# A decoder layer's opening rearranged: dummy matmuls, full-width rotary tables, kept zero columns, an earlier row-scale chain

## The chip, the cores and the metric

One core of a Trainium2 chip runs the kernel, in one launch. The metric is the device time of that launch in microseconds (us), on the core. TensorE (PE in the profile) multiplies matrices and loads their stationary operand (PEld), VectorE (DVE) and ScalarE (ACT) work on tiles of 128 partitions, GpSimd (POOL) fills and copies, and SyncE (SP) issues most transfers. Each engine works through its own instructions in order and waits on semaphores for the others.

## The reference

One layer of a decoder for 256 tokens of width 2048, in fp32, cut to what matters here:

```python
h = rms_norm(x, attn_norm_g)
proj = h @ w_in                               # 2048 x 4480
shifted = h + (prev_token - h) * mu           # of the 3360 columns of the first head group
y_rwkv = rwkv7_mixer(r, k, v, w, a, g, ...)   # 16 heads x 64: a recurrence over tokens
y_mla  = mla_mixer(c_q, c_kv, k_pe, positions, ...)   # 8 heads, a rotary key of 64 columns
x = x + concat(y_rwkv, y_mla) @ w_out
h = rms_norm(x, ffn_norm_g)
x = x + (silu(causal_conv3(h @ w_gate)) * (h @ w_up)) @ w_down     # width 5632
return rms_norm(x, final_norm_g)

def apply_rope(t, positions):
    inv_freq = ROPE_THETA ** (-arange(half) / half)           # half = 32
    ang = positions[..., None] * inv_freq
    return concat([t1 * cos(ang) - t2 * sin(ang), t2 * cos(ang) + t1 * sin(ang)])
```

The recurrence is computed in four chunks of 64 tokens, each with a small triangular system per head.

## The kernel before

**Exact products.** Every fp32 matrix is split into two parts, hi and lo, and the products of the parts are summed. Weights come in pieces of 512 KB. `piece` issues the transfer to a `raw` buffer on SP, ACT casts it to `hi` (L133), DVE subtracts to get `lo` (L134); there are three buffers of each kind. `prod_b` then makes eight matmuls of 512 columns with `hi` (L165: the activations' hi and lo side by side) and eight of 256 columns with `lo` (L168). `in_tile(i)` does this for two pieces and gives 128 columns of the input projection, transposed: 128 columns on partitions, 256 tokens free. `joined` adds the two halves (copy out by ACT L173, add by DVE L174, which frees the accumulator) and multiplies by `rsB`, the RMS norm's row scale (L175), since the matmuls work on x before its norm.

**Order of the projection.** 35 tiles: 0, 25 and 26 first (low-rank inputs, gates, rotary key), then key tiles 1 to 8, r tiles 9 to 16, v tiles 17 to 24, and the latents 27 to 34. Tiles 0, 25, 1 and 3 and most others accumulate in the PSUM pool `mm` (three buffers), 26 in `at` (two), and tile 2 in `ch` (three). So the third key tile, tile 3, needs a `mm` buffer that DVE's L174 must free.

**The opening.** The order of SP's transfers is the written order there (`manual_schedule`); on the other engines a scheduler that simulates the program sets each engine's order when the kernel is built. `xsplit` loads x transposed and splits it; `sums` loads x again and gets the sums of squares (`ssx`, ACT L317). `rsqrt` turns them into the row scale by three Newton steps on DVE (`rm`, `ry`, `rt`, L204 to L216), and `bcast` spreads it over partitions: two diagonal tiles `dg` (DVE L227), two matmuls with `ones` (PE L228, into `rsb`), and a copy to `rsB` (DVE L229). `rope_tables` makes the angles by a careful reduction on DVE (L255 to L281), 64 columns wide with four blocks of 32 frequencies stacked on partitions, takes Sin on ACT (L283 to L285), and 32 GpSimd operations (L291 to L295) spread them to `cosR` and `sinR`, 128 x 256.

**Behind it.** `shifted` joins a tile into a buffer `h` of 257 columns with a zero first column (a GpSimd memset each), and mixes each token with the one before it (ACT L377, DVE L378). `decay` makes the decays of two key tiles with Tanh and Exp (ACT L413 to L420) and a masked scan with `cmask` (DVE L418). When keys and r are there, Gram matrices go to DRAM and come back transposed (`dL`, `Lp`, SP L569), DVE solves the triangular systems row by row (L578 to L588), and the result makes another trip (`dT`, `dU`) to the matmuls `pR` (L628) and `pT` (L641). Projection work fills these waits on PE. Then come the four chunks (`px`, `XB`, `UV`, `pS`, `py`, L677 to L710), attention, the output projection and the FFN, where each of 44 rounds puts a gate tile into `gt`, 258 columns with two zero ones (a memset each).

Of the kernel before, what the change touches and what calls it, by code (L numbers as in the profile page):

```python
# [9 lines left out]
F32 = mybir.dt.float32  # L10
# [7 lines left out]
P = 128  # L18
# [17 lines left out]
    _o += _w  # L36
NVEC = _o

C_ID, C_MK, C_CAUS, C_BLK, C_INVF, NCST = 0, 128, 256, 384, 386, 387


def _two_pi_parts():
# [12 lines left out]
def hybrid_layer(ctx: ExitStack, tc: tile.TileContext, a: dict, out: bass.AP):  # L55
# [11 lines left out]
        uid[0] += 1  # L67
        return f"{s}{uid[0]}"

    NT2, NAT, NS4, NRAW, NHI, NLO, NMM, NCH, NT1 = 3, 2, 21, 3, 3, 3, 3, 3, 7  # L70

    def s4(dt=F32, n="s4"):
        return sb.tile([P, 1024], dt, tag="s4", name=nm(n), bufs=NS4)
# [170 lines left out]
    sinR = con([P, T], "sinR")  # L244

    def rope_tables():
        rp = [t2("rp", 384) for _ in range(2)]
        rp = [u[:, q * 64:(q + 1) * 64] for u in rp for q in range(4)]
        posi = rp.pop().bitcast(I32)
        nc.gpsimd.dma_start(posi, a["pos"])  # L250
        c1, c2, c3, c3r, c4r = _two_pi_parts()
        tpi = 2.0 * math.pi
        ang, k0, kh, lo, w = rp[:5]
        with tc.issue_after(last_x[0]):
            V.tensor_copy(ang, posi)  # L255
# [24 lines left out]
        fms(w, c3r)  # L280
        V.tensor_scalar(ang, ang, 3.1415925, -3.1415925, ALU.min, ALU.max)  # L281
        sn, cn = rp[5:7]
        S.activation(sn, ang, AF.Sin)  # L283
        S.activation(cn, ang, AF.Sin, scale=0.5)
        S.activation(cn, cn, AF.Square)  # L285
        V.tensor_scalar(cn, cn, -2.0, 1.0, ALU.mult, ALU.add)
        for b in range(4):
            bs = slice(b * 32, b * 32 + 32)
            for r in range(4):
                ro = slice(r * 32, r * 32 + 32)  # L290
                nc.gpsimd.tensor_copy(cosR[ro, b * 64:(b + 1) * 64], cn[bs])  # L291
                if r % 2:
                    nc.gpsimd.tensor_copy(sinR[ro, b * 64:(b + 1) * 64], sn[bs])
                else:
                    nc.gpsimd.tensor_scalar(sinR[ro, b * 64:(b + 1) * 64], sn[bs], -1.0, None, ALU.mult)  # L295
# [6 lines left out]

    ones = con([P, P], "ones")
    nc.gpsimd.memset(ones, 1.0)
# [14 lines left out]
    with tc.manual_schedule(engines={mybir.EngineType.SP}):  # L319
# [26 lines left out]
    hkk = con([P, 8], "hkk")
# [16 lines left out]
    with tc.issue_after(dve0):  # L363
        for b in (0, 2):
            V.tensor_copy(cmb[:, b * P:(b + 1) * P], cst[:, C_CAUS:C_CAUS + P])
        V.tensor_copy(idb, ident)
    cmask = t1("cmask")
    nc.gpsimd.memset(cmask, 1.0)
    nc.gpsimd.memset(cmask.rearrange("p (c t) -> p c t", t=64)[:, :, 0:1], 0.0)


    def shifted(acc, i, rows=slice(0, P), dst=None):
        h = t1("h", 257)
        nc.gpsimd.memset(h[rows, 0:1], 0.0)
# [3 lines left out]
        V.scalar_tensor_tensor(o[rows], h[rows, 0:256], vv("mu", i, rows), o[rows], ALU.mult, ALU.add)  # L378
        return o
# [7 lines left out]
    wa = shifted(acc0[0], 0)  # L387
    S.activation(wa[0:64], wa[0:64], AF.Tanh)
    shifted(acc0[1], 25, dst=sg1)
    sigmoid_(sg1)  # L390
# [561 lines left out]
    for blk, nf in enumerate((24, 20)):  # L952
        hh = [s4(F32R, "hh").rearrange("p (k t) -> p k t", k=4) for _ in range(nf // 4)]
        hl = [s4(F32R, "hl").rearrange("p (k t) -> p k t", k=4) for _ in range(nf // 4)]
        for fi in range(nf):
            f = f0 + fi
            accs = []
            for gu in range(2):
# [5 lines left out]
            nc.gpsimd.memset(gt[:, 0:2], 0.0)  # L964
# [46 lines left out]
def _consts():  # L1011
# [9 lines left out]
    c[64:128, C_BLK + 1] = 1.0  # L1021
    inv = (10000.0 ** (-np.arange(32, dtype=np.float64) / 32)).astype(np.float32)
    c[:, C_INVF] = np.tile(inv, 4)
    return c


def pack(inp):
# [62 lines left out]
```

## Time and profile before

| | |
|---|---|
| median of three timings | 1208.7 us (1202.65 to 1214.32) |
| span of the profiled execution | 1203.6 us (no separate time is listed for it) |
| mean granted TensorE clock | 0.991 |
| busy: PE, PEld, DVE, ACT, POOL | 1159.9, 990.6, 839.1, 599.4, 77.4 us |
| moved | 215.82 MB |

The profile's times start at the first instruction of the span. A row of a timeline gives start, duration, engine, source line, operation, output and inputs, and in brackets how long the engine had been idle and what released it. Durations of PE rows include the drain of the last matmul, so the distance to the next row is the better price. The row of transfers by stretch gives the granted clock of PE, the share of the 16 DMA engines' time, and GB/s.

### The profile page before, as it was taken

To read this page: it belongs to the slowest core of one execution; us is meant where nothing else is said; L and a number is where in the kernel's file an instruction comes from. 1 tells how busy PE (TensorE), PEld (TensorE's weight loads), DVE (VectorE), ACT (ScalarE), POOL (GpSimd) and SP (SyncE) were. 2 spreads that over 40 slices of the span, in tenths; PEclk is the share of its full clock that TensorE was granted. 3 is DMA by queue.
4 is the path that set the end of the run, shared out by engine and by line. 5 is a ranking of instruction groups with operands and counts; after the bars stand their busy time and mean duration, and the time that the engine had idled before them with its cause. 6 is when DMAs were issued, how large, how long until landed. Compare 5 with 4: busy or idle time off the path is not lost.

```text
span 1203.6 us, 18439 instructions
## 1 busy us (share of the span) xinstructions
PE 1159.9 (96%) x6993; PEld 990.6 (82%) x6993; DVE 839.1 (70%) x1352; ACT 599.4 (50%) x939; POOL 77.4 (6%) x214
## 2 busy tenths in 40 slices
PE   7899998998799999999999999999999999999996
PEld 6788877887577888888888888888888888888885
DVE  6898749977887556777777776444577777775563
ACT  6784434633444455655555554333455555554442
POOL 1500042002110001000000000000000000000000
PEclk9899998999999999999999999999999999999999
DMA  8555443754133555655555555555655555566662
GB/s 317 177 155 159 138 143 122 213 168 147 62 140 114 184 172 175 206 190 191 187 192 191 191 192 191 193 190 190 200 191 192 192 193 193 192 223 202 205 217 81
DMA packets 71017, 215.82 MB, mean 179 GB/s; under 512 B 17616, under 2 KB 17872, under 8 KB 70928
## 3 DMA queue, kind: packets, MB, share of 16 engines
q1 hardware_dynamic: 69776, 211.84, 53.9%
q10 hardware_dynamic: 768, 2.05, 0.5%
q8 instruction: 55, 0.90, 0.3%
q0 software_dynamic: 384, 0.75, 0.2%
q14 instruction: 34, 0.28, 0.1%
HBM read 210.48 MB, written 3.41 MB: 178 GB/s over the span
## 4 chain that ended last, share of the span: by engine, by line
PE 84%; DVE 8%; DMA 3%; POOL 2%; issue 1%; ACT 1%; SPq 1%; ACTq 0%; DVEq 0%; POOLq 0%
PE mm L165 34%; PE mm L168 17%; PE mm L185 9%; PE mm L187 9%; PE mm L186 9%; DVE lo L134 2%; PE pg L527 1%; DMA xt<-in_x 1%; PE px L677 1%; DMA Lp<-dL 1%; DMA raw<-in_win 0%; POOL cosR L291 0%; DMA dT<-Tq 0%; PE py L677 0%; SPq L540 0%
## 5 line engine op out<-in xcount | busy, mean ns | idle before, releaser
L134 DVE TENSOR_TENSOR lo<-raw,hi 128x1024 fp32r<-128x1024 f32 x368 | 453.0, 1231 | 288.0 <-ACT hi L133 283.1
L133 ACT CAST hi<-raw 128x1024 fp32r<-128x1024 f32 x376 | 395.5, 1052 | 451.7 <-issue 234.9
L165 PE MATMUL mm<-z,hi 128*128 128x512 f32 x1408 | 351.3, 392 | 0.0
L165 PEld LDWEIGHTS mm<-z,hi 128*128 128x128 f32 x1408 | 251.9, 188 | 43.7
L168 PEld LDWEIGHTS mm<-z,lo 128*128 128x128 f32 x1408 | 188.3, 188 | 14.5
L168 PE MATMUL mm<-z,lo 128*128 128x256 f32 x1408 | 191.6, 278 | 0.0
L165 PE MATMUL mm<-x,hi 128*128 128x512 f32 x528 | 144.4, 410 | 17.9 <-DVE h L174 9.6
L186 PE MATMUL mm<-lo,hh 128*128 128x512 f32 x336 | 130.7, 389 | 0.0
L187 PE MATMUL mm<-hi,hl 128*128 128x512 f32 x336 | 130.7, 389 | 0.0
L165 PEld LDWEIGHTS mm<-x,hi 128*128 128x128 f32 x528 | 97.0, 195 | 35.6 <-ACT hi L133 8.3
L185 PE MATMUL mm<-hi,hh 128*128 128x512 f32 x336 | 119.7, 389 | 0.0
L168 PEld LDWEIGHTS mm<-x,lo 128*128 128x128 f32 x528 | 74.7, 193 | 7.4 <-issue 1.0
L168 PE MATMUL mm<-x,lo 128*128 128x256 f32 x528 | 79.9, 288 | 0.0
L186 PEld LDWEIGHTS mm<-lo,hh 128*128 128x128 f32 x336 | 63.1, 188 | 13.1
L187 PEld LDWEIGHTS mm<-hi,hl 128*128 128x128 f32 x336 | 63.1, 188 | 13.1
L185 PEld LDWEIGHTS mm<-hi,hh 128*128 128x128 f32 x336 | 63.1, 188 | 13.0
L186 PE MATMUL mm<-lo,yhi 128*128 128x512 f32 x128 | 51.1, 399 | 0.0
L187 PE MATMUL mm<-hi,ylo 128*128 128x512 f32 x128 | 50.5, 394 | 0.0
L185 PE MATMUL mm<-hi,yhi 128*128 128x512 f32 x128 | 49.6, 405 | 0.0
L964 POOL MEMSET gt<- 128x2 f32 x44 | 4.3, 100 | 575.8 <-DVE hl L976 558.9
L187 PEld LDWEIGHTS mm<-hi,ylo 128*128 128x128 f32 x128 | 24.1, 188 | 5.6 <-DVE ylo L749 0.4
L185 PEld LDWEIGHTS mm<-hi,yhi 128*128 128x128 f32 x128 | 23.9, 188 | 5.7 <-DVE kn L174 0.8
(291 smaller groups left out, 1142.8 us busy)
## 6 DMA issues: line engine op xcount, KB each, us to landing
raw<-in_wgu SPq DMA_DIRECT2D x176, 512.0 KB, 3.3
raw<-in_wdn SPq DMA_DIRECT2D x88, 512.0 KB, 4.1
raw<-in_win SPq DMA_DIRECT2D x70, 512.0 KB, 3.7
raw<-in_wout SPq DMA_DIRECT2D x32, 512.0 KB, 3.4
raw<-in_wuq SPq DMA_DIRECT2D x6, 512.0 KB, 3.3
xraw<-in_xT SPq DMA_DIRECT2D x4, 512.0 KB, 6.3
xt<-in_x SPq DMA_DIRECT2D x4, 512.0 KB, 6.7
raw<-in_wuv SPq DMA_DIRECT2D x4, 512.0 KB, 3.3
```

The source lines that it names most:

```text
L133: S.copy(hi, raw)
L134: sub = (eng or V).tensor_tensor(lo, raw, hi.bitcast(F32), ALU.subtract).ins
L165: PE.matmul(acc, hi[:, j * P:(j + 1) * P], act(kt0 + j), start=first and j == 0, stop=False, skip_group_check=True)
L168: PE.matmul(acc[:, :T], lo[:, j * P:(j + 1) * P], act(kt0 + j)[:, 0, :], start=False, stop=last and j == n - 1, skip_group_check=True)
L185: PE.matmul(accs[tb], ah, wh, start=first and j == 0, stop=False)
L186: PE.matmul(accs[tb], ah, wl, start=False, stop=False)
L187: PE.matmul(accs[tb], al, wh, start=False, stop=last and j == n - 1)
L527: PE.matmul(pg[h][:, o:o + P], BK[pp][hs, gg, w * 2 + r, :, :], AR[pp][hs, gg, w * 2 + r, :, :], start=o == 0, stop=True, skip_group_check ...
L677: PE.matmul(dst[HS[h], a_ * 64:(a_ + 1) * 64], lhsT, rhs, start=n == 0 and a_ == 0, stop=True, skip_group_check=True)
L964: nc.gpsimd.memset(gt[:, 0:2], 0.0)
```

## The change

- Twenty matmuls `ones` x `ones` into an `at` buffer (`wps`) are written right behind the memset of `ones`.
- `rope_tables` works at 128 x 256: the positions (now one row of 256) are broadcast to all partitions by the transfer, ACT's Sin takes a sign per partition (`C_SGN`, a new column of the constants) and writes `sinR` itself, DVE writes `cosR`. The 32 GpSimd operations are gone. Its first working tiles lie in a tile `wide`.
- Two kept buffers `hb` of 260 columns have their first two columns zeroed once. `shifted` and the FFN use them in turn for `h` and `gt`; the memsets for each are gone, and the pool `t1` has five buffers instead of seven. `cmask`, `kraw`, `ksw` and the first shifted tile lie in a tile `early`, and `cmask` is filled at the start.
- The row scale is written ahead of the third key tile, and that tile, in a `ch` buffer, ahead of `rope_tables` and the transfer of `lora`.

```diff
@@ rope_tables
-        rp = [t2("rp", 384) for _ in range(2)]
-        rp = [u[:, q * 64:(q + 1) * 64] for u in rp for q in range(4)]
-        posi = rp.pop().bitcast(I32)
-        nc.gpsimd.dma_start(posi, a["pos"])
+        rp = [t2("rp", 384) for _ in range(3)]
+        wide = s4(n="rw")
+        posi = s4(n="rposi")[:, 0:T]
+        nc.gpsimd.dma_start(posi.bitcast(I32), a["pos"].broadcast_to([P, T]))
...
-        S.activation(sn, ang, AF.Sin)
+        S.activation(sinR, ang, AF.Sin, scale=cst[:, C_SGN:C_SGN + 1])
         S.activation(cn, ang, AF.Sin, scale=0.5)
         S.activation(cn, cn, AF.Square)
-        V.tensor_scalar(cn, cn, -2.0, 1.0, ALU.mult, ALU.add)
-        for b in range(4):
...
+        V.tensor_scalar(cosR, cn, -2.0, 1.0, ALU.mult, ALU.add)
@@ opening
     nc.gpsimd.memset(ones, 1.0)
+    wps = at("wps")
+    for _ in range(20):
+        PE.matmul(wps[:, :P], ones, ones, start=True, stop=True)
+    hb = [con([P, 260], f"hb{i}") for i in range(2)]
+    for u in hb:
+        nc.gpsimd.memset(u[:, 0:2], 0.0)
...
+    early = s4(n="early")
+    cmask = early[:, 3 * T:4 * T]
...
         kacc[1] = in_tile(2, ch)
+        rsB = sb.tile([P, T], F32, tag="rsB", name="rsB", bufs=1)
+        V.tensor_tensor(ssx[:, 0:2], ssx[:, 0:2], ssx[:, 2:4], ALU.add)
+        bcast(rsqrt(ssx[:, 0:2], 1.0 / DM, EPS, 2, V), rsB)
+        kacc[2] = in_tile(3, ch)
         rope_tables()
         lora = s4(n="lora")
         nc.sync.dma_start(lora, a["lora"])
...
-        h = t1("h", 257)
-        nc.gpsimd.memset(h[rows, 0:1], 0.0)
+        h = hbuf()[:, 1:258]
...
-            gt = t1("gt", 258)
-            nc.gpsimd.memset(gt[:, 0:2], 0.0)
+            gt = hbuf()
```

What this does to the engines' orders shows at three places. The first is DVE around the row scale: `ry` and `rt` are the last Newton steps, `dg` the diagonal tiles, `lo99` and `lo102` of before belong to the third key tile. Before:

```order
L134 TENSOR_TENSOR lo49_342<-raw47_339,hi48_341 128x1024
L216 SCALAR_TENSOR_TENSOR ry54_427<-rt55_428,ry54_427 128x2
L213 TENSOR_TENSOR rt55_428<-ry54_427 128x2
L214 TENSOR_TENSOR rt55_428<-rt55_428,rm53_426 128x2
L216 SCALAR_TENSOR_TENSOR ry54_427<-rt55_428,ry54_427 128x2
L227 TENSOR_SCALAR dg57_441<-cst_72,ry54_427 128x128
L227 TENSOR_SCALAR dg58_444<-cst_72,ry54_427 128x128
L134 TENSOR_TENSOR lo99_635<-raw97_632,hi98_634 128x1024
L134 TENSOR_TENSOR lo102_657<-raw100_654,hi101_656 128x1024
L229 COPY rsB_424<-rsb56_440 128x256
```

Of the change, where `lo61` and `lo64` belong to the third key tile and `rw` is the rope's working tile:

```order
L134 TENSOR_TENSOR lo61_417<-raw59_414,hi60_416 128x1024
L264 SCALAR_TENSOR_TENSOR rw68_461<-rw68_461 128x256
L213 TENSOR_TENSOR rt54_393<-ry53_392 128x2
L260 TENSOR_SCALAR rw68_461<-rw68_461 128x256
L134 TENSOR_TENSOR lo64_439<-raw62_436,hi63_438 128x1024
L214 TENSOR_TENSOR rt54_393<-rt54_393,rm52_391 128x2
L261 TENSOR_SCALAR rw68_461<-rw68_461 128x256
L216 SCALAR_TENSOR_TENSOR ry53_392<-rt54_393,ry53_392 128x2
L264 SCALAR_TENSOR_TENSOR rw68_461<-rw68_461 128x256
L274 TENSOR_SCALAR rw68_461<-rw68_461 128x256
L227 TENSOR_SCALAR dg56_406<-cst_72,ry53_392 128x128
L227 TENSOR_SCALAR dg57_409<-cst_72,ry53_392 128x128
```

The diagonal tiles stood ahead of the third tile's two subtractions and now stand behind both, with rope operations among them. The second place is PE behind the second key tile (`ch43` before, `ch45` in the change). Before:

```order
L168 MATMUL ch43_316<-x4_68,lo49_342 128x256 x4
L228 MATMUL rsb56_440<-dg57_441,ones_76 128x128
L228 MATMUL rsb56_440<-dg58_444,ones_76 128x128
L165 MATMUL mm96_631<-x1_65,hi98_634 128x512 x4
L165 MATMUL mm96_631<-x2_66,hi98_634 128x512 x4
```

Of the change:

```order
L168 MATMUL ch45_344<-x4_68,lo51_370 128x256 x4
L228 MATMUL rsb55_405<-dg56_406,ones_76 128x128
L165 MATMUL ch58_413<-x1_65,hi60_416 128x512 x4
L165 MATMUL ch58_413<-x2_66,hi60_416 128x512 x4
L168 MATMUL ch58_413<-x1_65,lo61_417 128x256 x4
L168 MATMUL ch58_413<-x2_66,lo61_417 128x256 x4
L165 MATMUL ch58_413<-x3_67,hi63_438 128x512
L228 MATMUL rsb55_405<-dg57_409,ones_76 128x128
```

The third tile has moved from a `mm` to a `ch` accumulator; the first row-scale matmul still stands ahead of it, and the second now stands inside it. The third place is PE at the first `pR` matmul behind the triangular solve. Before:

```order
L165 MATMUL mm457_3148<-x1_65,hi459_3151 128x512 x4
L165 MATMUL mm457_3148<-x2_66,hi459_3151 128x512 x4
L168 MATMUL mm457_3148<-x1_65,lo460_3152 128x256 x2
L628 MATMUL pR370_2267<-T11307_1894,G1191_1204 32x32
L628 MATMUL pR371_2302<-T11307_1894,G1193_1206 32x32
```

Of the change, where `rsb417` is the row scale of the first latent:

```order
L228 MATMUL rsb417_3024<-dg418_3025,ones_76 128x128
L228 MATMUL rsb417_3024<-dg419_3028,ones_76 128x128
L168 MATMUL mm440_3141<-x4_68,lo446_3167 128x256 x2
L165 MATMUL mm449_3195<-x1_65,hi451_3198 128x512 x4
L165 MATMUL mm449_3195<-x2_66,hi451_3198 128x512 x4
L168 MATMUL mm449_3195<-x1_65,lo452_3199 128x256 x4
L168 MATMUL mm449_3195<-x2_66,lo452_3199 128x256 x4
L165 MATMUL mm449_3195<-x3_67,hi454_3220 128x512 x4
L165 MATMUL mm449_3195<-x4_68,hi454_3220 128x512 x3
L631 MATMUL pR344_2206<-T11288_1847,G1179_1171 32x32
```

Ahead of the first `pR` PE starts its 65th piece of x times weights before, and its 70th in the change: five pieces of the latents have moved ahead of it. On ACT, the Sin of the tables comes behind the first Tanh, with five table loads in the program instead of three, and L173's copies of the first two accumulators stand ahead of the squares of `sums`. On SP, the third tile's two transfers stand ahead of `lora`.

More of the change, by code (lines that the diff above doesn't have):

```diff
@@ L37 @@
 NVEC = _o
-C_ID, C_MK, C_CAUS, C_BLK, C_INVF, NCST = 0, 128, 256, 384, 386, 387
+C_ID, C_MK, C_CAUS, C_BLK, C_INVF, C_SGN, NCST = 0, 128, 256, 384, 386, 387, 388
 def _two_pi_parts():
@@ L68, in nm @@
         return f"{s}{uid[0]}"
-    NT2, NAT, NS4, NRAW, NHI, NLO, NMM, NCH, NT1 = 3, 2, 21, 3, 3, 3, 3, 3, 7
+    NT2, NAT, NS4, NRAW, NHI, NLO, NMM, NCH, NT1 = 3, 2, 21, 3, 3, 3, 3, 3, 5
     def s4(dt=F32, n="s4"):
@@ L246, in rope_tables @@
     def rope_tables():
-        rp = [t2("rp", 384) for _ in range(2)]
-        rp = [u[:, q * 64:(q + 1) * 64] for u in rp for q in range(4)]
-        posi = rp.pop().bitcast(I32)
-        nc.gpsimd.dma_start(posi, a["pos"])
+        rp = [t2("rp", 384) for _ in range(3)]
+        wide = s4(n="rw")
+        posi = s4(n="rposi")[:, 0:T]
+        nc.gpsimd.dma_start(posi.bitcast(I32), a["pos"].broadcast_to([P, T]))
         c1, c2, c3, c3r, c4r = _two_pi_parts()
         tpi = 2.0 * math.pi
-        ang, k0, kh, lo, w = rp[:5]
+        ang, k0, kh, lo = (wide[:, i * T:(i + 1) * T] for i in range(4))
+        w, sn, cn = (u[:, :T] for u in rp)
         with tc.issue_after(last_x[0]):
-            V.tensor_copy(ang, posi)
+            V.tensor_copy(ang, posi.bitcast(I32))
         V.tensor_scalar(ang, ang, cst[:, C_INVF:C_INVF + 1], None, ALU.mult)
@@ L281, in rope_tables @@
         V.tensor_scalar(ang, ang, 3.1415925, -3.1415925, ALU.min, ALU.max)
-        sn, cn = rp[5:7]
-        S.activation(sn, ang, AF.Sin)
+        S.activation(sinR, ang, AF.Sin, scale=cst[:, C_SGN:C_SGN + 1])
         S.activation(cn, ang, AF.Sin, scale=0.5)
         S.activation(cn, cn, AF.Square)
-        V.tensor_scalar(cn, cn, -2.0, 1.0, ALU.mult, ALU.add)
-        for b in range(4):
[L288 to L295, printed above, removed]
+        V.tensor_scalar(cosR, cn, -2.0, 1.0, ALU.mult, ALU.add)
     def sigmoid_(t, rows=slice(0, P)):
@@ L304, in hybrid_layer, with hbuf @@
     nc.gpsimd.memset(ones, 1.0)
+    wps = at("wps")
[4 more added lines that the diff above has]
+        nc.gpsimd.memset(u[:, 0:2], 0.0)
+    hbn = [0]
+    def hbuf():
+        hbn[0] += 1
+        return hb[hbn[0] % 2][:, 0:258]
+    early = s4(n="early")
+    cmask = early[:, 3 * T:4 * T]
+    nc.gpsimd.memset(cmask, 1.0)
+    nc.gpsimd.memset(cmask.rearrange("p (c t) -> p c t", t=64)[:, :, 0:1], 0.0)
     warm = st("warm", 2)
@@ L339, in hybrid_layer @@
         nc.sync.dma_start(lora, a["lora"])
-    rsB = sb.tile([P, T], F32, tag="rsB", name="rsB", bufs=1)
-    V.tensor_tensor(ssx[:, 0:2], ssx[:, 0:2], ssx[:, 2:4], ALU.add)
-    bcast(rsqrt(ssx[:, 0:2], 1.0 / DM, EPS, 2, V), rsB)
     om_mu = con([P, 27], "om_mu")
@@ L366, in hybrid_layer @@
         V.tensor_copy(idb, ident)
-    cmask = t1("cmask")
-    nc.gpsimd.memset(cmask, 1.0)
-    nc.gpsimd.memset(cmask.rearrange("p (c t) -> p c t", t=64)[:, :, 0:1], 0.0)
     def shifted(acc, i, rows=slice(0, P), dst=None):
-        h = t1("h", 257)
-        nc.gpsimd.memset(h[rows, 0:1], 0.0)
+        h = hbuf()[:, 1:258]
         joined(h[rows, 1:257], acc, rsB, rows)
@@ L386, in hybrid_layer @@
         nc.gpsimd.memset(kpe[h], 0.0)
-    wa = shifted(acc0[0], 0)
+    wa = shifted(acc0[0], 0, dst=early[:, 2 * T:3 * T])
     S.activation(wa[0:64], wa[0:64], AF.Tanh)
@@ L430, in hybrid_layer @@
     acc = acc0[2]
-    kraw, ksw = t1("kraw"), t1("ksw")
+    kraw, ksw = early[:, 0:T], early[:, T:2 * T]
     joined(kraw[0:64], acc, rsB, slice(0, 64))
@@ L1023, in _consts @@
     c[:, C_INVF] = np.tile(inv, 4)
+    c[:, C_SGN] = np.repeat([-1.0, 1.0, -1.0, 1.0], 32)
     return c
@@ L1049, in pack @@
     o["gnw"], o["gnb"] = f["rwkv_gn_w"], f["rwkv_gn_b"]
-    pos = f["positions"].astype(np.int32).reshape(4, 1, 64)
-    o["pos"] = np.broadcast_to(pos, (4, 32, 64)).reshape(P, 64)
+    o["pos"] = f["positions"].astype(np.int32).reshape(1, T)
     def btiles(m):
```

## The prediction

> **What bounds the kernel now.** I read the busy times first, then the chain that ended last.
>
> ```profile
> span 1203.6 us, 18439 instructions
> PE 1159.9 (96%) x6993; PEld 990.6 (82%) x6993; DVE 839.1 (70%) x1352; ACT 599.4 (50%) x939; POOL 77.4 (6%) x214
> PE 84%; DVE 8%; DMA 3%; POOL 2%; issue 1%; ACT 1%; SPq 1%; ACTq 0%; DVEq 0%; POOLq 0%
> ```
>
> PE is busy for 1159.9 of 1203.6 us, so everything that is not PE work comes to 43.7 us, plus what PE loses at a lower clock. Only stretches in which PE waits or runs slowly can give anything. The busy time by stretch says where those are (the columns are PE, weight loads, DVE, ACT and POOL busy, then the granted clock):
>
> ```profile
> 0.00:8.00 8.00, 0.00 (x0) 0.00 (x0) 1.68 (x4) 4.01 (x7) 5.60 (x16) 1.00 0.76 274
> 8.00:14.00 6.00, 5.72 (x18) 4.85 (x19) 5.61 (x10) 5.46 (x11) 0.00 (x0) 1.00 1.03 393
> 39.00:42.00 3.00, 0.39 (x4) 0.20 (x2) 2.59 (x3) 1.70 (x3) 2.83 (x5) 0.91 0.80 205
> 42.00:48.00 6.00, 5.41 (x17) 4.67 (x18) 3.14 (x9) 3.72 (x8) 4.15 (x20) 0.50 0.52 167
> 49.00:91.00 42.00, 41.55 (x243) 34.66 (x242) 41.20 (x91) 35.94 (x69) 2.31 (x12) 1.00 0.49 144
> 242.00:275.00 33.00, 32.53 (x532) 28.69 (x531) 25.59 (x48) 15.36 (x28) 2.80 (x14) 1.00 0.54 167
> ```
>
> In the opening PE has nothing for 8 us, then runs dense, pauses near 39 to 42, and from 42 to 48 has a granted clock of 0.50. From 49 to 91 PE (41.55 of 42.00) and DVE (41.20) are both full. PE's own rows in order of time price the opening:
>
> ```profile
> 8.28 2.08 PE L165 MATMUL mm<-x,hi 128*128 128x512 f32 x4 [8.28 <-ACT hi L133]
> 24.97 2.00 PE L165 MATMUL at<-x,hi 128*128 128x512 f32 x8
> 26.81 1.11 PE L168 MATMUL at<-x,lo 128*128 128x256 f32 x8
> 36.01 1.99 PE L165 MATMUL ch<-x,hi 128*128 128x512 f32 x8
> 37.84 1.11 PE L168 MATMUL ch<-x,lo 128*128 128x256 f32 x8
> 38.78 0.61 PE L228 MATMUL rsb<-dg,ones 128*128 128x128 f32 x4
> 42.59 3.75 PE L165 MATMUL mm<-x,hi 128*128 128x512 f32 x8 [3.20 <-DVE h L174]
> 46.14 1.91 PE L168 MATMUL mm<-x,lo 128*128 128x256 f32 x8
> ```
>
> At 24.97 eight matmuls take 1.84 us up to the next row, and with the eight of L168 (0.94) half a tile takes 2.78; a tile of two pieces is 5.55. At 8.28 only four take about as long as those eight, although the granted clock reads 1.00 there: I call this the first slow stretch, by durations alone. It lasts until about 14.1, 5.85 us, and at half speed it loses about **2.9 us**. At 42.59 the same eight take 3.55 up to the next row, beside a granted clock of 0.50: the slow stretch from 42.59 to 48.26 loses about **2.8 us**. The wait ahead of it, from about 39.2, is **3.35 us**. These three, 9 us or 0.75% of the span, are what the opening holds for PE.
>
> **The change, part by part.** *Dummy matmuls.* Twenty fp32 matmuls of 128x128 on `ones`. The tile is ready early, and an operation of the same kind is shown by the four rows of L228 above (two calls, 0.61 us with their drain, 0.305 a call at most) and by a bare pair (one call) between two others:
>
> ```profile
> 0.81 0.20 POOL L304 MEMSET ones<- 128x128 f32 x1
> 172.15 0.38 PE L547 MATMUL pt<-cst,BK 128*128 128x128 f32 x2
> 172.29 0.48 PE L165 MATMUL mm<-x,hi 128*128 128x512 f32 x1
> 33.25 1.05 ACT L133 CAST hi<-raw 128x1024 fp32r<-128x1024 f32 x1 [0.61 <-DMA raw<-in_win]
> 34.33 1.28 DVE L134 TENSOR_TENSOR lo<-raw,hi 128x1024 fp32r<-128x1024 f32 x1 [0.31 <-ACT hi L133]
> ```
>
> The pair issues in 0.14 us, so one call is 0.14 to 0.305 at speed and twice that when slow. I take 0.22 and 0.44. From 1.1 us a slow stretch of the same 5.85 us holds 13.3 calls, the other 6.7 take 1.5, and the last ends near 8.4: just where PE is first wanted. At 0.305 the end is near 10.0, 1.7 us late but fast; at 0.14 it is 6.6 and PE idles again. If the warm state holds, the 2.9 us come back, but only as far as the inputs allow: the last piece of the second key tile has its hi from 33.25 to 34.30 after a wait on its DMA and its lo until about 35.5, so with no backlog PE ends that tile at 34.3 + 1.84 + 0.94 = 37.1 at the earliest, against 38.78. So the dummies move this point by -1.6 us (bounds: -1.7 and, if they run late and nothing is warm, +1.7).
>
> The Trainium skill ("TensorE: Matmul & The Clock Gate", Part 1) gives a half-rate default, full rate after a busy window of about 3.4 us, and half rate again after an idle window of that length. By it the dummies would warm PE a little sooner than my 5.85 us; the pause of 3.35 us above, after which the granted clock is 0.50, agrees with its second half.
>
> *Row scale and third key tile.* The idea of the order is that the third tile of keys fills the pause, since its `ch` accumulator is free while `mm` waits for DVE's L174. But the first row-scale matmul now stands ahead of it on PE, and its `dg` on DVE stands behind both lo's of that same tile (rows shown with the change). The rows of before at that place:
>
> ```profile
> 36.35 0.48 DVE L227 TENSOR_SCALAR dg<-cst,ry 128x128 f32<-128x128 f32 x2
> 36.81 1.23 DVE L134 TENSOR_TENSOR lo<-raw,hi 128x1024 fp32r<-128x1024 f32 x1
> 39.41 1.22 DVE L134 TENSOR_TENSOR lo<-raw,hi 128x1024 fp32r<-128x1024 f32 x1 [1.38 <-PE rsb L228]
> 40.55 0.42 DVE L229 COPY rsB<-rsb 128x256 f32<-128x256 f32 x1
> 38.33 1.05 ACT L133 CAST hi<-raw 128x1024 fp32r<-128x1024 f32 x1 [1.56 <-DMA raw<-in_win]
> 46.44 0.49 DVE L378 SCALAR_TENSOR_TENSOR sh<-h,vec,sh 128x256 f32<-128x256 f32 x1 [1.96 <-POOL h L374]
> 50.64 0.28 DVE L300 TENSOR_SCALAR sg<-sg 128x256 f32<-128x256 f32 x1
> ```
>
> The lo at 39.41 is the second of the third tile: its cast at 38.33 waited 1.56 us for its transfer, and the transfer waits for a `raw` buffer, not for PE. The lora transfer (512 KB) no longer stands ahead of it on SP, so I let it land up to 1 us sooner: that lo ends between 39.5 and 40.6. Behind it, ahead of `dg`, come two small steps of the row scale and four rope operations (0.16, 0.28, 0.16, 0.48 and 0.28 by the rows above and their like), some 1.5 us, then `dg` 0.25: first `dg` at 41.2 to 42.3, its matmul, and the third tile at **41.6** (41.0 to 42.2) instead of 42.59. PE, done with the second tile at 37.2, waits 4.4 us instead of 3.35, and goes slow again: the 2.8 us stay. Net for the opening: **-1.0 us** (bounds: -5.4 without the wait and -2.8 more without the slow stretch, +2 if that transfer comes later). Queued behind the waiting `dg` on DVE are the later lo's; rsB itself now needs the second row-scale matmul, inside the third tile, and comes near 48 instead of 40.55.
>
> *Rope at full width.* Some 24 DVE operations go from 64 to 256 columns. At 64 they took about 4.7 us, in gaps of DVE before 30.7; at 256 (0.28 for one input as at 50.64, 0.49 with a second tensor as at 46.44, less about 0.08 that successive ones overlap) they take 8.0: +3.3. About 5.9 us of them now stand behind the third tile's lo's, where DVE has no gap until 91. The pauses that GpSimd caused DVE go (1.96 at 46.44), since the 32 copies are gone:
>
> ```profile
> 39.58 6.42 POOL L291 COPY cosR<-rp 32x64 f32<-32x64 f32 x16
> 46.31 0.28 POOL L374 MEMSET h<- 128x1 f32 x3
> 44.96 1.28 ACT L388 ACT_TABLE_LOAD   x1
> L964 POOL MEMSET gt<- 128x2 f32 x44 | 4.3, 100 | 575.8 <-DVE hl L976 558.9
> ```
>
> DVE's key stage therefore ends some 4 to 7 us later (it ended at 96.7), but PE needs less of it: ACT copies the first accumulators out early (L173 now stands ahead of the squares), so the next two tiles find their `mm` slots without rsB. I cost it at 0 to PE; without that cover it is +3.3, and +7.5 if the whole lateness of rsB came through. The position transfer (128 KB instead of 32) stands behind the GpSimd memsets that end at 6.5 and is wanted after 31: nothing.
>
> *Activation tables.* Sin is now evaluated behind the first Tanh, so ACT loads tables twice more: 2 x 1.28 = 2.57 us by the row. ACT is busy 35.94 of 42.00 from 49 to 91, so 6 us of idle time hide it: 0, at most +2.57.
>
> The Trainium skill ("ScalarE: Activation LUTs", What ACT_TABLE_LOAD costs) puts a switch at about 2.66 us with its drain, and so speaks against this part. By it the two loads cost 5.3 us, an estimate that ACT's idle time would still hold; the rows of before show the load alone.
>
> *Kept zero columns.* The 44 memsets of 0.1 us ended their waits on DVE, 558.9 us of idle POOL: they hide now. Two `hb` buffers serve rounds of some 11 us of PE work in the FFN, whose `gt` is read within its round: 0, bounds 0 and 0.3 a round if a round did wait (44 rounds, +13), which I hold for excluded, as one round's use of `gt` is a few us of DVE and ACT work.
>
> *What the order moves later.* The chain through the triangular solve:
>
> ```profile
> 175.82 6.07 DMA Lp<-dL
> 184.05 3.78 PE mm L165 x8
> 231.87 5.64 DMA dT<-Tq
> 242.44 2.21 PE pR L628 x124
> 274.51 0.85 DVE L688 TENSOR_TENSOR XB<-px,mtok 64x256 f32<-64x256 f32 x2
> ```
>
> PE stops for 6.2 us ahead of 184.05, while Lp comes back and DVE can't free `mm`. The new order allows one tile (5.55) more before that stop, but the last gram product stands 2.7 us of PE work later, so its transfer does too, and one raw piece fewer is ahead of it: the stop stays near 5.9, -0.3. Then the order puts five more pieces of projection work ahead of `pR` (rows shown with the change), 5 x 2.78 = 13.9 us: it moves from 242.44 to about 255.0 (+13.9, -1.0, -0.3). The stage from `pR` to the second chunk's XB took 32.07 us, in which PE was busy 32.53 of 33 only because that work lay in it. With 13.9 us less to fill it, it takes 18.2 plus perhaps 1.5 that the filler had covered, 19.7. XB then comes at 274.7, against 274.51; bounds 273 and 276.5. From there on DVE's order is the same in both.
>
> **Sum:** opening -1.0, solve -0.3, filler +1.5: **+0.2** on a span of 1203.6, thus 1203.8. No time beside the span is listed for the profiled execution; the timings (1202.65, 1208.7, 1214.32) straddle it, the median 5.1 above. Forecast 1203.8 + 5.1 = **1209**, bounds of this case 1201 to 1217.
>
> **The rivals.** *The pause really goes.* If the third tile's second piece lands 4 us sooner, `dg` is ready by 37.4, PE doesn't stop, and 5.2 (42.59 to 37.4) and 2.8 come back; with the stop ahead of the solve shrinking by up to 5.5 too, that is -8 to -13.5: 1195.5 to 1201. For it: DVE's pauses go. Against it: the cast at 38.33 waited on a DMA, and a DMA share of 0.80 at 39 to 42 leaves little to speed up.
>
> *Slower: the filler runs out.* If the stage from `pR` on is held by DVE and the round trips among px, XB, UV and pS, not by the filler, it still takes up to 32 us, and XB comes 12.5 us late: 1222. It decides above 19.7 us of stage, and each us above that costs one. For it: DVE was busy 25.59 of 33 there. Against: five lo's and the joins of that filler, some 8 us of those 25.6, leave with it.
>
> *The dummies do nothing.* The granted clock is 1.00 even before 14, so what halves the first matmuls may not be the clock; then only -1.0 is at stake, since the wait for `dg` swallows it: 1208 to 1210.
>
> **How the numbers follow.** A difference under about 1% (12 us) can't be told from none here. The forecast 0.55, the dummies' rival 0.08 (same time), the pause going 0.22 (its upper part within 1%, 0.17 beyond), the filler running out 0.15 (0.13 beyond). That gives faster 0.17, same 0.70, slower 0.13. The range goes to 1194 below and 1222 above: it takes in both rivals' prices, and leaves out a round-by-round wait in the FFN.
>
> **What would show it.** Right: the second tile's last matmuls near 37, a PE pause of 4 to 5 us ending at an L228 matmul near 41.5, granted clock near 0.5 behind it; five table loads on ACT; `pR` near 255 and the second chunk's XB near 275, with PE idle between them. Wrong: no pause at 37 to 42, a first matmul after 10, `pR` below 250, or XB outside 272 to 278.

## The result: 0.59% slower, and where the time went

The changed kernel takes 1217.99 us in the median of 14 runs (1214.1 to 1219.62), the kernel before 1210.64 us in 14 runs: a ratio of **1.0059** (95% interval 1.0043 to 1.0075), some 7 us. The forecast was 1209 us and "no difference over 1%", with 1194 to 1222 as the range. The time lies inside it, but the 7 us have a cause that no step of the prediction names. Three lines of the page of the changed kernel (span, busy time, chain that ended last):

```profile
span 1217.9 us, 18248 instructions
PE 1181.6 (97%) x7033; PEld 1010.7 (83%) x7033; DVE 835.6 (69%) x1352; ACT 602.2 (49%) x941; POOL 60.7 (5%) x113
PE 86%; DVE 7%; DMA 2%; ACT 2%; issue 1%; POOL 1%; SPq 0%; ACTq 0%; DVEq 0%; POOLq 0%
```

PE's busy time went up by 21.7 us. The dummies are 6.4 of that; the rest is the same work done more slowly. POOL lost 16.7 us and DVE 3.5, and neither shows in the time. The stretches that answer to those of before, with the stage behind the solve last:

```profile
8.00:14.00 6.00, 5.75 (x31) 4.72 (x32) 5.30 (x10) 4.70 (x11) 0.00 (x0) 1.00 1.02 365
38.00:41.00 3.00, 0.72 (x6) 0.52 (x5) 2.58 (x9) 0.91 (x2) 0.00 (x0) 1.00 0.91 350
41.00:46.00 5.00, 5.00 (x22) 4.40 (x23) 3.38 (x8) 1.57 (x2) 0.00 (x0) 0.66 0.59 210
70.00:80.00 10.00, 8.51 (x34) 7.13 (x34) 10.00 (x26) 8.86 (x20) 0.00 (x0) 0.66 0.34 124
253.00:281.00 28.00, 22.96 (x447) 20.83 (x447) 17.23 (x33) 8.49 (x20) 0.00 (x0) 0.76 0.33 100
```

Between 8 and 14 PE now gets 31 matmuls done instead of 18: it starts fast. Up to 281 us there are three slow stretches instead of the one that was expected: at 41 to 46 (granted clock 0.66), at 70 to 80 (0.66), and at 253 to 281 (0.76), where PE is busy for only 22.96 of 28 us. In PE's and DVE's rows of the opening and of the solve:

```profile
8.19 1.20 PE L165 MATMUL mm<-x,hi 128*128 128x512 f32 x4 [0.73 <-ACT hi L133]
37.44 1.11 PE L168 MATMUL ch<-x,lo 128*128 128x256 f32 x8
40.83 0.49 PE L228 MATMUL rsb<-dg,ones 128*128 128x128 f32 x2 [2.28 <-DVE dg L227]
41.08 2.87 PE L165 MATMUL ch<-x,hi 128*128 128x512 f32 x8
240.69 1.16 DVE L591 COPY tp<-Tq 128x1024 f32<-128x1024 f32 x1
253.03 2.21 PE L631 MATMUL pR<-T,G 32*32 32x32 f32 x124
280.48 0.84 DVE L691 TENSOR_TENSOR XB<-px,mtok 64x256 f32<-64x256 f32 x2
```

The third key tile starts at 41.08 (42.59 before), behind a wait for `dg`. The second chunk's XB comes at 280.48 against 274.51: 6.0 us late. Those 6.0 are not all of the 14.3 us between the two spans. Another 2.1 come between there and the FFN, whose first gate product starts at 475.6 us against 467.6. (The two profiles also lie far apart by chance: the change's is the slowest of its 14 runs, 1219.62 us, and a second profile of before, below, has a span of 1206.5.) In the FFN, at full clock and with no wait of PE, one round of gate and up products takes longer. The rows count ACT's first operation on the convolution, one a round, in a window of the second FFN block; first those of before, then those of the change:

```profile
L967 ACT ACTIVATE cv<-gt,vec x17: 593/596/603, 894.9 to 1071.3; 128x256 f32<-128x256 f32 x17
```

```profile
L969 ACT ACTIVATE cv<-hb,vec x17: 598/601/604, 895.4 to 1074.2; 128x256 f32<-128x256 f32 x17
```

Sixteen rounds from the first start to the last are 176.4 us before and 178.8 now: **11.03 and 11.18 us a round**, 0.15 us more. From the first gate product to the last up product, which takes in all 44 rounds, it is 617.1 us before (467.6 to 1084.7) and 623.4 now (475.6 to 1099.0): **6.2 us more**. PE's rows show it in single pieces, before and after, as the distance from each row to the next:

```profile
702.36 1.11 PE L168 MATMUL mm<-z,lo 128*128 128x256 f32 x8
703.31 2.00 PE L165 MATMUL mm<-z,hi 128*128 128x512 f32 x8
705.14 1.07 PE L168 MATMUL mm<-z,lo 128*128 128x256 f32 x8
706.05 1.99 PE L165 MATMUL mm<-z,hi 128*128 128x512 f32 x8
```

```profile
702.21 1.11 PE L168 MATMUL mm<-z,lo 128*128 128x256 f32 x8
703.16 2.00 PE L165 MATMUL mm<-z,hi 128*128 128x512 f32 x8
705.00 1.12 PE L168 MATMUL mm<-z,lo 128*128 128x256 f32 x8
705.95 2.00 PE L165 MATMUL mm<-z,hi 128*128 128x512 f32 x8
```

The two pieces take 3.70 us from 702.36 to 706.05 before, and 3.74 from 702.21 to 705.95 now. Such differences are lost in the mean durations of a page, and a PE that is 100% busy gives no wait to read. In the FFN's code the change touched nothing but `gt`'s buffer.

### The profile page after: what moved, and what is told of

The parts are those of the page before. It is cut to its first block, busy times and chain, and to the rows that moved or that the text cites. A ratio compares the mean times of both kernels' runs of the same rounds, so it can differ in the third digit from the quotient of the medians.

```text
span 1217.9 us, 18248 instructions
## 1 busy us (share of the span) xinstructions
PE 1181.6 (97%) x7033; PEld 1010.7 (83%) x7033; DVE 835.6 (69%) x1352; ACT 602.2 (49%) x941; POOL 60.7 (5%) x113
## 4 chain that ended last, share of the span: by engine, by line
PE 86%; DVE 7%; DMA 2%; ACT 2%; issue 1%; POOL 1%; SPq 0%; ACTq 0%; DVEq 0%; POOLq 0%
PE mm L165 34%; PE mm L168 18%; PE mm L187 9%; PE mm L185 9%; PE mm L186 9%; DVE lo L134 1%; PE pg L530 1%; DMA xt<-in_x 1%; PE py L680 1%; PE px L680 1%; DVE tm L585 1%; DMA xraw<-in_xT 1%; DMA Lp<-dL 0%; PE pT L644 0%; ACT hi L133 0%
## 5 line engine op out<-in xcount | busy, mean ns | idle before, releaser
L168 PEld LDWEIGHTS mm<-z,lo 128*128 128x128 f32 x1408 | 192.1, 190 | 13.7
L168 PE MATMUL mm<-z,lo 128*128 128x256 f32 x1408 | 196.3, 282 | 0.0
L165 PE MATMUL mm<-x,hi 128*128 128x512 f32 x512 | 135.8, 401 | 2.7 <-ACT hi L133 2.0
L186 PE MATMUL mm<-lo,hh 128*128 128x512 f32 x336 | 130.7, 389 | 0.0
L187 PE MATMUL mm<-hi,hl 128*128 128x512 f32 x336 | 130.7, 389 | 0.0
L165 PEld LDWEIGHTS mm<-x,hi 128*128 128x128 f32 x512 | 92.0, 191 | 20.7 <-ACT hi L133 2.8
L168 PE MATMUL mm<-x,lo 128*128 128x256 f32 x512 | 77.2, 288 | 0.1
L168 PEld LDWEIGHTS mm<-x,lo 128*128 128x128 f32 x512 | 71.3, 192 | 6.0 <-DVE lo L134 0.5
L187 PE MATMUL mm<-hi,ylo 128*128 128x512 f32 x128 | 50.2, 393 | 0.0
L174 DVE TENSOR_TENSOR hb<-mm,hb 128x256 f32<-128x256 f32 x68 | 28.4, 419 | 0.1
```

The lines of the kernel that those rows point to most:

```text
L165: PE.matmul(acc, hi[:, j * P:(j + 1) * P], act(kt0 + j), start=first and j == 0, stop=False, skip_group_check=True)
L168: PE.matmul(acc[:, :T], lo[:, j * P:(j + 1) * P], act(kt0 + j)[:, 0, :], start=False, stop=last and j == n - 1, skip_group_check=True)
L174: V.tensor_tensor(dst, acc[rows, :T], dst, ALU.add)
L186: PE.matmul(accs[tb], ah, wl, start=False, stop=False)
L187: PE.matmul(accs[tb], al, wh, start=False, stop=last and j == n - 1)
```

## The experiments

Twelve runs follow, in four groups, the first of them the kernel before again; ratios are to the kernel before, on the same chip, with 95% intervals. The groups ran on different chips, so versions of different groups are compared by their ratios. The diffs are excerpts. My theory for the first group was that the loss lay in the order (DVE's solve and the chunk stage behind it); the rival there was the opening. The FFN's pace was the second question.

**The kernel before once more.** No edit.

> The kernel of before, unchanged, for a second profile. Theory (the FFN rounds of the two profiles, 11.03 and 11.17 us, differ because of where the kept buffers put the other tiles): rounds of 11.03 us again, span near 1204. Rival (the length of a round varies from run to run of one program): rounds between 11.03 and 11.17 us, span up to 1210.

One run, 1208.27 us, span 1206.5. Its row for the FFN rounds reads as before's does (897.7 to 1074.1 for 17): 11.03 us again. So the pace belongs to the program. The opening does vary: its third key tile starts at 41.23 with no slow stretch behind it,

```profile
41.23 2.07 PE L165 MATMUL mm<-x,hi 128*128 128x512 f32 x8 [2.81 <-DVE h L174]
```

eight matmuls to the next row in 1.91 us, where the first profile had 3.55 behind a wait of 3.20. So a pause of about 3 us (2.81 here, 3.20 there) was followed by a slow stretch in one execution of this program and not in the other. The first gate product of the FFN starts at 470.4 us here, 2.9 later than in the first profile; the versions below that keep before's orders have it at 469.9 to 471.7.

**The dummies alone.**

```diff
     nc.gpsimd.memset(ones, 1.0)
+    wps = at("wps")
+    for _ in range(20):
+        PE.matmul(wps[:, :P], ones, ones, start=True, stop=True)
```

> Before plus the twenty dummy matmuls alone. Theory (PE starts fast, and the wait for rsB at 39 to 42 swallows the gain): second key tile done near 37 instead of 38.8, its wait for L174 again until 42 to 42.6, total within 2 us of before. Rival (2.9 us are really saved): 3 us faster than before.

1208.73 us, ratio 1.0009 (0.9989 to 1.0028).

```profile
8.24 1.19 PE L165 MATMUL mm<-x,hi 128*128 128x512 f32 x4 [0.59 <-ACT hi L133]
40.34 2.08 PE L165 MATMUL mm<-x,hi 128*128 128x512 f32 x8 [2.11 <-DVE h L174]
```

The first matmuls run fast, and PE again waits for L174 later. The theory's bound holds: nothing that can be measured.

**The filler behind pR.** In the changed kernel:

```diff
-            acc = in_tile(27 + x * 4 + j)
+            if x == 1 and j >= 2:
+                with tc.issue_after(pR_last):     # last matmul of L631
+                    acc = in_tile(27 + x * 4 + j)
+            else:
+                acc = in_tile(27 + x * 4 + j)
```

> The changed kernel with the last two latent tiles (33 and 34, four pieces) held behind the last pR matmul. Theory (the four pieces more in the solve lengthen DVE's solve and leave the chunk stage without filler, idle and at half clock): pR near 246 instead of 253, XB of the second chunk at 275 to 277 instead of 280.5, total 4 to 6 us less than the changed kernel. Rival (the time is lost in the opening and at 71 to 79, and the filler's place is indifferent): pR earlier, XB still near 280, total within 1.5 us of the changed kernel.

1224.19 us, 1.0137 (1.0115 to 1.0159): worse than the change (1.0059), so my theory fell in this form. PE's two largest waits from 40 to 250 (us in total, times, longest):

```profile
PE rsb L228 <- DVE dg L227: 6.5, 2, 4.3
PE pR L631 <- DMA T<-dU: 4.7, 2, 4.2
```

Only PE's part was held; DVE did the same 16 subtractions inside the solve, whose last copy came at 238.1. PE had nothing left at 239, waited twice, and then ran the solve's small matmuls at a granted clock of 0.50 (249 to 262). XB came at 286.2. The filler ahead of `pR` had been covering DVE's time, not costing PE any.

**The row scale first on DVE.** In the changed kernel:

```diff
-        kacc[2] = in_tile(3, ch)
-        rope_tables()
+        with tc.issue_after(last_dg[0]):          # second dg of bcast, DVE L227
+            kacc[2] = in_tile(3, ch)
+            rope_tables()
```

> The changed kernel with DVE's row-scale steps and dg kept ahead of the third key tile's two subtractions and of the rope. Theory (the third tile waits only because dg stands behind those subtractions): no pause of PE at 38 to 41, no slow clock at 41 to 45, rsB near 42 instead of 47; 4 us gained by 48, of which DVE's full stretch from 49 to 91 gives back half or more: total 0 to 4 us less than the changed kernel. Rival (the pause is the third tile's own transfer): the pause stays within 1 us, total unchanged.

1217.91 us, 1.0077 (1.0053 to 1.0101), no gain over the change.

```profile
37.77 0.38 PE L228 MATMUL rsb<-dg,ones 128*128 128x128 f32 x2
37.91 1.64 PE L165 MATMUL ch<-x,hi 128*128 128x512 f32 x6
69.88 3.75 PE L165 MATMUL mm<-x,hi 128*128 128x512 f32 x8 [2.09 <-DVE hb L174]
```

The step is shown: `dg`'s place made the pause, which is gone, and the third tile starts at 37.91 instead of 41.08. But the 3.2 us come back as a wait for L174 at 67.5 and a slow stretch behind it (eight matmuls take 3.75 us with their drain, where 2.0 are usual), since DVE is full there (busy for 10.00 of 10 us from 60 to 70).

**Place of the weights' buffers, in both directions.** In the compiled programs `hi` begins at byte 153952 of a partition before and at 156064 in the change: the two kept buffers (1056 bytes each, 2112 in all) lie ahead of it, and the `t1` pool that shrank lies behind. `z` and the first part of x begin at 16544 in both. Two kernels differ from their parents in place alone (and, the second, in two memsets on POOL). The `raw` buffers, the working tiles ahead of them and what lies behind move along with `hi` and `lo`; x, `z` and the constants up to `ones` stay:

```diff
     ones = con([P, P], "ones")                    # of the kernel before
+    sg1, sg2 = con([P, T], "sg1"), con([P, T], "sg2")
+    nkk, hkk = con([P, 8], "nkk"), con([P, 8], "hkk")   # moved up from further down
```

> Before with four constant tiles (sg1, sg2, nkk, hkk; 2112 bytes a partition) created ahead of the weights' buffers, so that raw, hi and lo lie where the changed kernel has them; every engine's order is that of before. Theory (the pace of the FFN's matmuls hangs on where hi and lo lie): rounds of 11.17 us instead of 11.03, the gate and up products 6.2 us longer, total 6 us over before. Rival (the pace comes from what the changed kernel runs beside them, the kept buffers or the missing memsets): rounds of 11.03, total within 1.5 us of before.

```diff
-    hb = [con([P, 260], f"hb{i}") for i in range(2)]    # of the changed kernel,
+    hb = [con([P, 260], f"hb{i}") for i in range(2)]    # now behind the opening
```

> The changed kernel with its two kept buffers created behind the weights' buffers, so that raw, hi and lo lie where before has them; orders of the changed kernel but for the two memsets. Theory (place of hi and lo): rounds of 11.03 us, total 6 us under the changed kernel, 1212. Rival (the kept buffers' use): rounds of 11.17, total unchanged at 1218.

Before with the moved buffers: 1216.14 us, **1.0059** (1.0039 to 1.0080). The change with before's place: 1210.29 us, **1.0004** (0.9983 to 1.0024). Their rounds, in that order:

```profile
L967 ACT ACTIVATE cv<-gt,vec x16: 597/599/601, 900.9 to 1068.5; 128x256 f32<-128x256 f32 x16
```

```profile
L970 ACT ACTIVATE cv<-hb,vec x16: 595/600/602, 900.4 to 1065.8; 128x256 f32<-128x256 f32 x16
```

167.6 and 165.4 us for 15 rounds, 11.17 and 11.03. Moving the buffers makes a loss as large as the change's without any other part of it, and moving them back takes the loss away, within intervals of about 0.2%. The use of `hb`, the missing memsets and the orders leave the pace alone.

**DVE's subtractions out of the solve.** In the changed kernel, the tiles 32 to 34:

```diff
+            if x == 1 and j >= 1:
+                with tc.issue_after(last_tp[0]):  # the copy tp<-Tq, DVE L591
+                    acc = in_tile(27 + x * 4 + j)
```

> The changed kernel with DVE's subtractions of the last three latent tiles (32 to 34) queued behind the solve's last copy: 12 subtractions between the solve's first product and that copy instead of 16 (before has 11). Theory (what delays the chunks is DVE's solve, lengthened by those subtractions): that copy at 236 instead of 240.7, pR near 248 instead of 252.5, the second chunk's XB near 276.5 instead of 280.5, total 3 to 5 us under the changed kernel. Rival (the chunk stage takes as much longer as pR comes sooner, as PE's order there is full): XB within 1.5 us of 280.5, total within 1.5 us of the changed kernel.

1214.09 us, 1.0040 (1.0022 to 1.0058), 0.19% under the change's ratio, though the two intervals overlap.

```profile
235.02 1.10 DVE L592 COPY tp<-Tq 128x1024 f32<-128x1024 f32 x1
274.88 0.85 DVE L692 TENSOR_TENSOR XB<-px,mtok 64x256 f32<-64x256 f32 x2
```

The copy came 5.7 us sooner and XB 5.6, as the theory had it and a little more. Of the 5.7, 4.1 arise inside the solve (51.5 us from `Lp`'s product on DVE to that copy, 55.6 in the change); the rest had come about ahead of it. In its corrected form the theory stands, and the other profiles bear it out: that stretch takes 49.6 to 50.2 us with 11 subtractions in it (before twice, with the dummies, with moved buffers, with the order alone), 51.3 to 51.5 with 12, and 55.5 to 56.2 with 16. What delays the chunks is DVE's work inside the solve.

**The third tile's order alone**, on the kernel before (the two hunks of the change on `rsB` and `kacc[2]`).

> Before with the row scale ahead of the third key tile and that tile in a ch buffer ahead of the rope, nothing else: 3 table loads, 64 pieces ahead of pR, 11 subtractions in the solve. Theory (the losses of the changed kernel come from the place of hi and lo and from DVE's solve, neither of which this has): PE's pause at 38 to 42 falls under 1.5 us, total 0 to 5 us under before. Rival (moving the third tile is itself what costs): total 3 us or more over before.

1215.47 us, 1.0047 (1.0025 to 1.0069), with rounds of 11.03: the rival. Three lines, PE at 70 to 80 us and the second chunk:

```profile
70.00:80.00 10.00, 8.21 (x28) 6.41 (x28) 9.06 (x24) 9.16 (x22) 0.20 (x2) 0.58 0.34 107
77.27 3.78 PE L165 MATMUL mm<-x,hi 128*128 128x512 f32 x8 [0.50 <-DVE h L174]
282.81 0.85 DVE L689 TENSOR_TENSOR XB<-px,mtok 64x256 f32<-64x256 f32 x2
```

The pause at 38 to 42 is gone, but PE is busy for only 8.21 of 10 us from 70 to 80 at a granted clock of 0.58, and from `pR` at 242.7 to XB there are 40 us against 32. The new order has 64 pieces ahead of `pR`, one fewer than before, and runs its `pT` and first `px` at a clock of 0.66 (250 to 260).

**Which distance counts.** The kernel before with an unused tile of 64 and of 32 bytes a partition ahead of the weights' buffers; every order of PE, DVE, ACT and SP stays.

```diff
     ones = con([P, P], "ones")
+    gap = con([P, 16], "gap")                     # 8 in the second
+    nc.gpsimd.memset(gap[:, 0:1], 0.0)
```

> Before with an unused tile of 64 bytes a partition ahead of the weights' buffers, orders as before. The distance from the activations' buffers (z, x) to hi and lo becomes a multiple of 256 bytes, as it is in the changed kernel; in before it leaves 192. Theory (what counts is that distance modulo 256): FFN rounds of 11.17 us, total 6 to 7 us over before, from 64 bytes alone. Rival (a larger unit, as 4 KB, counts, or the distance to other tiles): rounds within 0.05 us of 11.03, total within 2 us of before.

> The same with 32 bytes: the distance leaves 224 modulo 256. Theory (only equal addresses modulo 256 are slow): rounds of 11.03 us, total within 2 us of before. Rival (any step away from before's place is slower, or 32-byte steps count): rounds over 11.1 us, or under 10.95.

64 bytes: 1213.79 us, 1.0026 (1.0010 to 1.0042). 32 bytes: 1217.83 us, 1.0060 (1.0047 to 1.0073). Their rounds:

```profile
L969 ACT ACTIVATE cv<-gt,vec x16: 597/599/601, 901.6 to 1069.2; 128x256 f32<-128x256 f32 x16
```

```profile
L969 ACT ACTIVATE cv<-gt,vec x16: 593/598/602, 903.6 to 1072.0; 128x256 f32<-128x256 f32 x16
```

11.17 and 11.23 us a round. 64 bytes are enough for exactly the change's pace, so the unit is small, as the theory said; but 32 bytes give a slower one still, so equal addresses modulo 256 are not the only slow ones. The 64-byte kernel's timed difference, 3.1 us with 5.1 at the interval's end, is under the 6.2 us that its own profile shows from the first gate product to the last up product (470.6 to 1094.0, as long as in the change); that is left open.

**Tables and kept buffers alone**, on before's place of hi and lo, without dummies, row scale and third tile as before.

> Before with the full-width rotary tables and the kept buffers alone (created behind the weights' buffers, so hi and lo lie as in before), without the dummies and with the row scale and third key tile as in before: 3 table loads, 16 subtractions in the solve, 68 pieces ahead of pR. Theory (the parts add up: the whole at this place of hi and lo is 0.5 us over before, the order of the third tile alone 6.5 us over): 5 to 6 us under before. Rival (what counts is the schedule that each version gets, above all the 16 subtractions in the solve): 0 to 5 us over before.

1210.61 us, 1.0007 (0.9991 to 1.0022): the rival. The parts do not add up: 0.07% for this one, 0.47% for the order alone, 0.04% for both with the dummies. Each version gets a schedule of its own. Here Lp's product comes at 177.13, 4.8 us sooner than before; the solve with its 16 subtractions then takes 55.75 us instead of 50.2, and XB comes at 273.31. PE from 70 to 80 us, where the order alone was slow:

```profile
70.00:80.00 10.00, 10.00 (x61) 8.36 (x61) 10.00 (x24) 9.11 (x20) 0.00 (x0) 1.00 0.34 107
```

**Three places in one kernel.** The change with both gains, and a gap of 192 bytes between the pairs of `hi` and `lo`:

```diff
+            k = nth[0] % 3
+            if k and nth[0] < 3:
+                nc.gpsimd.memset(con([P, 48], f"gap{k}")[:, 0:1], 0.0)
+            nth[0] += 1
-            hi = sb.tile([P, 1024], F32R, tag="hi", name=nm("hi"), bufs=NHI)
+            hi = sb.tile([P, 1024], F32R, tag=f"hi{k}", name=nm("hi"), bufs=1)   # lo alike
```

> The changed kernel with the kept buffers behind the weights' buffers (as in the run that gained 0.55% on it) and the subtractions of tiles 32 to 34 behind the solve's last copy; and the three pairs of hi and lo at three distances from z modulo 256 bytes: 192, 128 and 64. The pairs take turns, so the FFN's pace by pair tells the three apart. Theory (128 and 64 are as good as 192; slow are 0 and 224): 229 and 116 ns from matmul to matmul (512 and 256 columns) for all three pairs, both gains add up, 1206 to 1209, 0 to 0.3% under before. Rival (192 is the best of all): two of three pairs slower by 1.5 to 5 ns, total 3 to 6 us more than that.

1221.03 us, 1.0099 (1.0070 to 1.0127). PE in the FFN, three pieces and the next one's first half:

```profile
901.68 1.99 PE L172 MATMUL mm<-z,hi 128*128 128x512 f32 x8
903.51 1.10 PE L175 MATMUL mm<-z,lo 128*128 128x256 f32 x8
904.45 2.02 PE L172 MATMUL mm<-z,hi 128*128 128x512 f32 x8
906.32 1.10 PE L175 MATMUL mm<-z,lo 128*128 128x256 f32 x8
907.26 2.02 PE L172 MATMUL mm<-z,hi 128*128 128x512 f32 x8
909.12 1.07 PE L175 MATMUL mm<-z,lo 128*128 128x256 f32 x8
910.03 1.99 PE L172 MATMUL mm<-z,hi 128*128 128x512 f32 x8
```

For the pairs at 192, 128 and 64 eight hi matmuls take 1.83, 1.87 and 1.86 us, eight lo matmuls 0.94, 0.94 and 0.91. That is 2.77, 2.81 and 2.77 us a piece. None beats 192, where before happened to lie; 128 is the slowest, and 64 is as fast in sum: slower with `hi`, faster with `lo`. So the rival holds for one pair of two. Its price is passed all the same, by 6 us and more, for a reason that neither side named. Up to the first gate product (470.4 us) this run is level with the second profile of before; from there to the end it takes 747.3 us against 736.1. Only half of those 11 us lie in the gate and up products. The other half lies in the products by `w_down`, which stream `hi` and `lo` past the split activations `hh` and `hl`: between the last up product of the first block and the first gate product of the second, before takes 130.7 us and this run 133.8.

So no version that was run beats the kernel before beyond its interval. The two gains together with all pairs at 192 were not run; by the ratios above (1.0004, less the 0.19% of the solve's edit) that would be 0.15% under the kernel before, less than the half-width of the intervals here, and the 470.4 us of this run promise no more than a tie.

## Why the prediction was right in its number and wrong in its reasons

That the number held is luck in good part. "No difference over 1%" and a range of 28 us had room for a loss of 7.4 us that the sum (+0.2) does not contain, and its terms were off in both directions.

- **What it left out: where tiles lie.** "*Kept zero columns* ... 0" priced the buffers' instructions and waits, and these did cost nothing. It had no term for the 2112 bytes by which they move `hi` and `lo`; such a move alone measured 1.0059. Without that the whole change is 1.0004 (0.9983 to 1.0024), which agrees with the forecast's sum of +0.2 us, though not with the terms in it: there errors cancel.
- **Dummies.** Right that the wait behind them swallows them (1.0009), and that they end the first slow stretch. The granted clock of 1.00 ahead of 14 us, which spoke against the clock, is no record: the first record of the clock in before's trace is at 14.1 us, where that stretch ends, and in the change's at 4.6. The end at 8.4 was 7.5. The gain at the second tile's end was 0.4 us on the first profile of before, not 1.6: PE now waits for inputs on the way, 0.73 us at 8.19 and twice more before 28.
- **Row scale and third tile.** Right at the place itself: PE waits for `dg`, the third tile starts at 41.08 (41.6 forecast), and the clock drops behind it. By the Trainium skill ("TensorE: Matmul & The Clock Gate", Part 1) that takes an idle window of about 3.4 us; here PE issued nothing from about 38.4 to 40.83, 2.4 us, and the rows from 41 to 46 have a granted clock of 0.66, so here the measurement decides for less. It is not so in each execution: with the same orders on before's place PE issued nothing for 2.8 us up to 40.69, and the clock stayed at 1.00 from 41 to 46. The net of -1.0 is not borne out: this order alone, in a schedule of its own, measured 1.0047.
- **Rope and tables: "0 to PE".** PE's two waits near 72 and the slow stretch at 70 to 80 cost about 5 us in the change, and with them went the lead of the third tile:

```profile
58.69 1.28 ACT L416 ACT_TABLE_LOAD   x1
72.01 1.13 PE L463 MATMUL ssP<-cst,ksq 128*128 128x2 f32 x8 [0.67 <-ACT ta L417]
73.84 3.75 PE L165 MATMUL mm<-x,hi 128*128 128x512 f32 x8 [0.70 <-DVE hb L174]
```

  The cover that I named, ACT's idle time and the early copies, was there on average and not at 72. But the runs lay this stretch to the third tile's order rather than to the tables: with that order and the old tables PE is as slow there (8.21 us busy of 10, clock 0.58), with the new tables alone it is not (10.00 us busy, clock 1.00). That run waits earlier instead, near 51 to 56, and starts its 21st piece of the projection at 80.84 us, where the two profiles of before have 81.20 and 80.35: for the tables alone "0" holds. How much the two more table loads of the whole change add is not shown. The last of three loads starts there at 58.69 and the next operation at 59.98, 1.29 us; the rows show no drain of 1.4 us beside it, as the Trainium skill ("ScalarE: Activation LUTs", What ACT_TABLE_LOAD costs) would have it.
- **Solve.** "The stop stays near 5.9" was wrong: it went altogether, and with it the slow stretch behind it: 6.2 us gained, and 2.0 more (the piece behind the stop took 4.79 us before, from 184.05 to 188.84, where 2.76 is usual). "Filler +1.5" was wrong too. `pR` came at 253.0 (255.0 forecast), but the stage behind it took 27.4 us, not 19.7. With the cover gone there are waits in the stage (PE busy for 22.96 of 28 us), and the granted clock fell too (0.76 over it). The rival on the slower side had this place right, at half its price: XB is 6.0 us late, not 12.5. The same orders on before's place have XB 3.9 us sooner:

```profile
276.60 0.84 DVE L692 TENSOR_TENSOR XB<-px,mtok 64x256 f32<-64x256 f32 x2
```

  That is 2.1 us behind before. But 1.5 of the 3.9 are the slow stretch at 41 to 46, which that execution does not have (the third tile's first half takes 2.87 us there and 4.37 in the change), so at most some 2.4 of the 6.0 are left for `hi`'s and `lo`'s place.
- Of the other rivals, the pause did not go, and the dummies did speed the first matmuls.

## What to carry to other kernels

When a change adds or moves a kept tile, compare the addresses of the operands that the densest matmuls read, ahead of and behind the change, and measure the pace of these matmuls over many of them; a PE at 100% hides a few nanoseconds a matmul in every other view. To separate that from a change's own effect, move the tiles alone, with all orders kept. And a part of a schedule can't be priced alone when a scheduler sets the order: its parts here cost 0.07%, 0.47% and 0.09%, and together 0.04%.

## What the runs showed of the hardware that I had not expected

The pace of a stream of fp32 matmuls hung on where its operands lie in the partition, to 32 bytes. With `z` fixed and `hi` and `lo` moved together, a round of 32 + 32 matmuls took 11.03 us at a distance that leaves 192 modulo 256, 11.17 to 11.18 at 0 (for 64 bytes and for 2112 bytes of shift alike), and 11.23 at 224. In those runs `raw`, the working tiles and what lies behind moved too; that the pair's own place counts is shown by the last run, whose three pairs differ in one execution.

Whether it is the distance or the place itself is not settled, but the products by `w_down` point to the distance. Their activations `hh` and `hl` lie among the tiles that moved along, and the stretch of 130.7 us between the two blocks is as long with 2112, 64 or 32 bytes of shift as before; it grew to 133.8 only where the pairs of `hi` and `lo` were moved against `hh` and against each other. Nor does the distance modulo 256 tell the whole: over all its FFN pieces the pair at 192 of the last run takes 2.77 us where before takes 2.76. What in the chip makes the difference, no run here shows.

The Trainium skill ("TensorE: Matmul & The Clock Gate", Step-by-step: what each phase is for) says that loading the next tile's weights takes no SBUF read bandwidth from the running matmul. These runs do not decide that: the pace changes by 1 to 2% with the place, but reads of weights are not told apart from the other traffic beside them.
